# Order of the transposes and place of one division in a banded attention, on one Trainium2 core

## Chip, cores and metric

The kernel runs on one core of one Trainium2 chip. The metric is the device time of one execution in microseconds (us); for several runs their median is given. TensorE does the matrix products and the transposes, VectorE (DVE) and ScalarE (ACT) work on their results, GpSimd (POOL) does some of the splitting, and SyncE (SP) issues most of the loads.

## What is computed

A trunk of two layers over a prompt of 2048 positions and a sample of 512, with 1024 channels. The first layer is an attention in a window: every block of 128 queries sees its own block of keys and the two beside it, as far as they exist. The change lies in this layer:

```python
scores = einsum('bnqhgd,bnkhd->bnhgqk', qb, kw) * scale + bias      # three key blocks per query block
scores = where(mask, scores, -inf)
m = maximum(max(scores), sink)
p = exp(scores - m)
p = p / (sum(p) + exp(sink - m))
o = einsum('bnhgqk,bnkhd->bqnhgd', p, v)
x = x + (o * silu(gate)) @ w_out
```

The second layer mixes by a Fourier transform over positions and channels. It takes no part in the change.

## The kernel before

**Chunks.** The attention works in five chunks of 512 positions (`CHUNKS`, L35): chunk 0 is the whole sample, chunks 1 to 4 are the quarters of the prompt. Each chunk has four query blocks (0 to 3) and eight head pairs. A block has three key blocks (384 keys), except at an end of its sequence, where it has two (256 keys, `span`, L460). Block 0 is narrow in chunks 0 and 1, block 3 in chunks 0 and 4. For chunk 0 the weights are loaded in float32, split into a high and a low part (a cast on ScalarE, L121, and a subtraction on GpSimd, L126) and stored for the later chunks.

**Periods.** The loop of L851 runs n from 0 to 16; I call one pass a period. In period n one head pair and one pair of blocks is new (the lower pair, blocks 0 and 1, in even periods, the upper pair, blocks 2 and 3, in odd ones), and that of period n - 1 is old. The instructions of an engine follow a written order for those that go through `seq` and `pe` (L140 to L147); others, such as the weight casts, the squares for the next chunk's norm (L169) and the scaling of a projection (L299), have no written place, and a scheduler puts them between. In a period:

- TensorE makes the scores of one new block, `one`, into the banks `spt[0]` and `spt[1]` (L472), transposes the probabilities of an old block (`transp`, L517), makes the scores of the other new block, `two`, into `spt[2]` and `spt[3]`, and transposes the second old block. Then come projection matmuls for later head pairs (L95, as many as `quota`, L829, says) and the products of probabilities and values (`av`, L557).
- The transposes write two banks, one for each half of the queries. The block that is transposed second (an odd `b`) writes one half into `spt[0]` (L525), so it must wait until the new block's first scores have been read from there.
- VectorE adds bias to scores and takes the minimum on the way (`biased`, L491), makes the reciprocal of the sums (L507), divides three of the four heads (L511 in the prompt's chunks, L515 in chunk 0), makes the low part of the transposed probabilities (L540), and evicts projections and outputs (L410, L575).
- ScalarE makes the exponentials (`exps`, L499), divides the fourth head (L509), copies the transposed probabilities (`parts`, L539), and makes the first half of an eviction (L409 for queries, L566 for outputs).

**Order of the blocks.** `one` is the narrower block of the pair (L867 to L869), so the upper pair of chunks 0 and 4 is scored as 3, 2. The transposes and copies take the pair as 2, 3 all the same. ScalarE's division is that of the second head of the even block (L508): of the block scored first in most pairs, but of the one scored second in those upper pairs.

The queries of a head pair are evicted in odd periods, behind the divisions (L409 on ScalarE, then L410 on VectorE), and the next period's scores need them.

The functions that the change touches, with the profile's line numbers:

Of the kernel before, what the change touches and what calls it, by code (L numbers as in the profile page):

```python
# [42 lines left out]
def encoder(  # L43
# [33 lines left out]
    def bank(name):  # L77
        return banks[-1].tile([P, 512], F32, tag="bank", name=name)
# [61 lines left out]
    def seq(engine, ins):  # L140

        after(ins, chain.get(engine))
        chain[engine] = ins
        return ins

    def pe(ins):
        return seq(PE, ins) if PE in chain else ins  # L147

    def attention_phase():

        with ExitStack() as es:
# [88 lines left out]
            ps = bank("idle")  # L240
# [193 lines left out]
            def attention(c, p, res, uTs):  # L434
# [25 lines left out]
                def span(b):  # L460
                    gb = tok // P + b
                    k0 = 1 if tok + b * P == lo_t else 0
                    k1 = 2 if tok + (b + 1) * P == hi_t else 3
                    return gb, k0, k1
# [35 lines left out]
                        s[:, e0:e1], s[:, e0:e1], AF.Exp, bias=s[:, 386:387], scale=-1.0, accum_out=s[:, 387:388]  # L500
                    ))

                def divide(b, j):
                    gb, k0, k1 = span(b)
                    s = st[b, j]
                    ks, den = slice(1 + k0 * P, 1 + k1 * P), s[:, 387:388]
                    seq(DVE, DVE.reciprocal(den, den))  # L507
                    if j > b % 2:  # L508
                        seq(ACT, ACT.activation(s[:, ks], s[:, ks], AF.Copy, scale=den))  # L509
                    elif c:  # L510
                        seq(DVE, DVE.tensor_scalar(s[:, ks], s[:, ks], den, None, ALU.mult))  # L511
                    else:


                        seq(DVE, DVE.tensor_scalar(s[:, ks], s[:, ks], den, None, ALU.mult, ALU.add, accum_out=s[:, 386:387]))  # L515

                def transp(b):  # L517

                    gb, k0, k1 = span(b)
                    ss = [st.pop((b, j)) for j in range(2)]  # L520
                    if b % 2 == 0:
                        st["pts"] = ap.tile([P, 2, 2, 3, 2, P], F32R, align_bytes=LINE, tag="pt", bufs=1, name=f"pts{c}_{p}_{b}")
                    ps = [bank(f"pt{c}_{p}_{b}_{h}")[:, :384] for h in range(2 - b % 2)]
                    if b % 2:
                        ps.append(spt[0][:, 2:386])  # L525
                    ps = st["pt", b] = [t.rearrange("p (k j q) -> p k j q", k=3, j=2) for t in ps]
                    for j in range(2):
                        for kb in range(k0, k1):
                            for h in range(2):
                                rows = slice(64 * h, 64 * h + 64)  # L530
                                pe(PE.transpose(  # L531
                                    ps[h][:, kb, j, :], ss[j][rows, 1 + kb * P : 1 + (kb + 1) * P], ident[rows, rows]
                                ))
# [55 lines left out]
                def width(b):  # L589
                    gb, k0, k1 = span(b)  # L590
                    return k1 - k0

                return start, sinks, width, scores, biased, exps, divide, transp, parts, av, out_evac

            def out_proj(c, uTs):
# [198 lines left out]
            for c in range(len(CHUNKS)):  # L794
# [40 lines left out]
                def extra(i):  # L835
                    nonlocal norm_steps, invb, inv
                    if c + 1 < len(CHUNKS):
                        if i == 24:
                            norm_steps = stats(c + 1)
                        if i >= (38 if c else 24) and i % (2 if c else 4) == 0 and norm_steps:  # L840
                            inv = norm_steps.pop(0)()
                        elif i == 56:
                            invb = spread(c + 1, inv)
                    if c in EXTRA and i in EXTRA[c]:
                        EXTRA[c][i]()
                    if c == len(CHUNKS) - 1 and i in AHEAD:
                        AHEAD[i]()
                    if c == 0 and i % 8 == 3 and 1 <= i // 8 < 3:
                        load_w(0, LATE[i // 8 - 1], f"late{i // 8}", late=last_exp[0])

                for n in range(17):  # L851
                    new = (at[n // 2], 2 * (n % 2)) if n < 16 else None
                    old = (at[(n - 1) // 2], 2 * ((n - 1) % 2)) if n else None
                    behind = None
                    if c == 0 and n in (8, 10):

                        fetches[n // 2 + 2]()
                        behind = last_fetch[0]
                    if n % 2 == 0 and n < 14:
                        at[n // 2 + 1].start(behind)  # L860
                    if n % 2 and n // 2 + 2 < 8:
                        loads[n // 2 + 2]()
                    chain.setdefault(PE, None)

                    if new:

                        one, two = new[1], new[1] + 1  # L867
                        if new[0].width(two) < new[0].width(one):
                            one, two = two, one  # L869
                        new[0].scores(one, spt[:2])  # L870
                    if old:
                        old[0].transp(old[1])
                    if new:
                        for j in range(2):
                            new[0].biased(one, j)
                        new[0].scores(two, spt[2:])
                    if old:
                        old[0].transp(old[1] + 1)
                    if n == 15:

                        for j in range(2):
                            new[0].biased(two, j)
                    if old:
                        for b in range(2):
                            old[0].parts(old[1] + b)
                    if new:
                        for j in range(2):
                            new[0].exps(one, j)
                    if split and c:
                        split()  # L890
                        split = None
                    if new:
                        if n < 15:
                            for j in range(2):
                                new[0].biased(two, j)
                        while late:
                            late.pop()()
                        new[0].divide(one, 0)
                        for j in range(2):
                            new[0].exps(two, j)  # L900
                        new[0].divide(one, 1)
                        for j in range(2):
                            new[0].divide(two, j)
                    for i in range(quota[2 * n] if n < 15 else 18 - n):
                        (work or op).pop(0)()
                    if split:
                        split()
                        split = None
                    if old:
                        old[0].av(old[1])  # L910
                        split = old[0].out_evac(old[1])
                    if n % 2 and n < 15:
                        at[n // 2 + 1].sinks()
                    for i in range(4 * n, 4 * n + 4):
                        extra(i)
                    if n == 16:
                        split()
                    half = quota[2 * n + 1] if n < 14 else 4 if n == 14 else 2
                    for i in range(half):
                        (work or op).pop(0)()  # L920
# [770 lines left out]


    fourier_phase(attention_phase())


# [96 lines left out]
```

## Time and profile before

| | |
|---|---|
| median of three runs | 1588.2 us (1588.07 to 1588.9) |
| profiled execution | 1587.64 us |
| its span (first to last instruction) | 1585.9 us |
| granted TensorE clock, mean | 0.999 of full speed |
| instructions | 27430 |
| HBM read, written | 280.84 MB, 91.26 MB |

Times in the profile are microseconds from the start of the span unless marked ns. PE is TensorE's matrix products and PEld its weight loads, which overlap them. A row of the timeline gives start, duration, engine, line, operation, the tiles as out<-in, shape and count, and in brackets how long the engine had been idle and what ended that. A row of the waits gives who waited for whom, the sum in us, how often, and the longest wait. Matrix products are pipelined and their ends are modelled, so the shares of TensorE say little about short waits; the starts of instructions do.

### The profile page before, as it was taken

To read this page: it belongs to the slowest core of one execution; us is meant where nothing else is said; L and a number is where in the kernel's file an instruction comes from. 1 tells how busy PE (TensorE), PEld (TensorE's weight loads), DVE (VectorE), ACT (ScalarE), POOL (GpSimd) and SP (SyncE) were. 2 spreads that over 40 slices of the span, in tenths; PEclk is the share of its full clock that TensorE was granted. 3 is DMA by queue.
4 is the path that set the end of the run, shared out by engine and by line. 5 is a ranking of instruction groups with operands and counts; after the bars stand their busy time and mean duration, and the time that the engine had idled before them with its cause. 6 is when DMAs were issued, how large, how long until landed. Compare 5 with 4: busy or idle time off the path is not lost. (4 is left out here: it accounts for less than half of the span.)

```text
span 1585.9 us, 27430 instructions
## 1 busy us (share of the span) xinstructions
PE 1572.4 (99%) x9743; PEld 1320.2 (83%) x9743; DVE 1151.0 (73%) x2785; ACT 876.4 (55%) x2089; POOL 446.5 (28%) x613
## 2 busy tenths in 40 slices
PE   9999999999999999999999999999999999999998
PEld 7778888888898888988888888888888888888886
DVE  5788665887548786378764577669878878889796
ACT  6688634677237684257852476646655554343342
POOL 2566651421403414024222242223112111111110
PEclk9999999999999999999999999999999999999999
DMA  7587696665865567656649656675557469548752
GB/s 288 205 311 282 237 350 211 228 237 199 294 224 205 208 249 257 238 196 229 242 168 334 217 209 225 247 252 199 207 200 262 176 224 406 180 173 313 265 205 80
DMA packets 100579, 373.88 MB, mean 236 GB/s; under 512 B 12139, under 2 KB 22379, under 8 KB 83036
## 3 DMA queue, kind: packets, MB, share of 16 engines
q1 hardware_dynamic: 81708, 297.91, 52.8%
q0 software_dynamic: 16400, 70.04, 11.5%
q10 hardware_dynamic: 2336, 4.20, 0.7%
q8 instruction: 77, 1.26, 0.3%
q14 instruction: 58, 0.48, 0.1%
HBM read 280.84 MB, written 91.26 MB: 235 GB/s over the span
## 5 line engine op out<-in xcount | busy, mean ns | idle before, releaser
L95 PE MATMUL gp<-h,wg 128*128 128x512 f32 x960 | 237.7, 396 | 0.0
L95 PE MATMUL qp<-h,wq 128*128 128x512 f32 x960 | 237.2, 396 | 0.0
L491 DVE CUSTOM_DVE_ANT_0 S<-spt,b 128x385 f32<-128x385 f32 (+1 forms) x320 | 156.5, 528 | 103.7 <-PE spt L472 69.2
L95 PEld LDWEIGHTS gp<-h,wg 128*128 128x128 f32 x960 | 174.9, 188 | 37.3 <-issue 1.0
L95 PEld LDWEIGHTS qp<-h,wq 128*128 128x128 f32 x960 | 174.9, 188 | 36.7 <-issue 0.3
L499 ACT ACTIVATE S<-S 128x385 f32<-128x385 f32 (+1 forms) x320 | 188.8, 596 | 21.0 <-DVE S L491 20.6
L539 ACT CAST pts<-pt 128x384 fp32r<-128x384 f32 (+1 forms) x240 | 101.4, 461 | 166.2 <-PE pt L531 157.5
L540 DVE TENSOR_TENSOR pts<-pt,pts 128x384 fp32r<-128x384 f32 (+1 forms) x240 | 114.7, 524 | 20.5 <-ACT pts L539 19.5
L581 POOL TENSOR_TENSOR uT<-o,uT 128x256 fp32r<-128x256 f32 x75 | 55.6, 741 | 233.1 <-ACT uT L580 233.0
L95 PE MATMUL spt<-wo,uT 128*128 128x512 f32 x480 | 120.4, 391 | 0.0
L472 PE MATMUL spt<-kwin,qab 64*128 64x384 f32 (+1 forms) x960 | 119.1, 353 | 1.2 <-ACT qab L409 0.6
L95 PE MATMUL op<-wo,uT 128*128 128x512 f32 x480 | 118.9, 391 | 0.0
L557 PEld LDWEIGHTS av<-pts,v 128*128 128x128 f32 x576 | 101.3, 188 | 19.2 <-DVE pts L540 0.4
L557 PE MATMUL av<-pts,v 128*128 128x512 f32 (+1 forms) x576 | 116.0, 341 | 0.1
L95 PE MATMUL fo<-wo,tTu 128*128 128x512 f32 x480 | 115.2, 392 | 0.0
L95 PEld LDWEIGHTS op<-wo,uT 128*128 128x128 f32 x480 | 89.4, 188 | 18.5
L95 PEld LDWEIGHTS spt<-wo,uT 128*128 128x128 f32 x480 | 89.1, 188 | 18.4
L95 PEld LDWEIGHTS fo<-wo,tTu 128*128 128x128 f32 x480 | 88.3, 188 | 17.1
L511 DVE TENSOR_SCALAR S<-S 128x384 f32<-128x384 f32 (+1 forms) x192 | 96.0, 500 | 6.8
L472 PEld LDWEIGHTS spt<-kwin,qab 64*128 64x128 f32 x960 | 74.8, 186 | 30.0 <-issue 25.0
L577 POOL TENSOR_TENSOR o<-o,s 128x256 f32<-128x256 f32 x75 | 55.4, 738 | 137.4 <-DVE o L575 137.1
L531 PE MATMUL pt<-ident,S 64*128 64x64 f32 x1344 | 81.8, 222 | 0.0
(321 smaller groups left out, 3185.8 us busy)
## 6 DMA issues: line engine op xcount, KB each, us to landing
wo<-wsd SPq DMA_DIRECT2D x32, 1024.0 KB, 5.6
wq<-wsd SPq DMA_DIRECT2D x31, 1024.0 KB, 7.4
wg<-wsd SPq DMA_DIRECT2D x31, 1024.0 KB, 5.7
x<-x1d SPq DMA_DIRECT2D x40, 512.0 KB, 3.4
b<-b21d SPq DMA_DIRECT2D x40, 512.0 KB, 6.3
b<-rowd SPq DMA_DIRECT2D x40, 384.0 KB, 4.3
xs<-in_x_dram SPq DMA_DIRECT2D x23, 512.0 KB, 6.7
s2d<-gt POOLq DMA_DIRECT2D x40, 256.0 KB, 5.0
```

The source lines that it names most:

```text
L95: pe(PE.matmul(out, a[i], b[j], start=start and i + j == 0, stop=stop and i == 1, skip_group_check=more))
L472: pe(PE.matmul(banks[j][:, 2 + k0 * P : 2 + k1 * P], res["q"][rows, qp, b * P : (b + 1) * P], kwin[g][rows, kp, b * P + k0 * P : b * P + k ...
L491: seq(DVE, DVE.tensor_tensor_reduce(out=s[:, e0:e1], in0=ps[:, 1 + e0 : 1 + e1], in1=st["bias"][:, j, 386 - e1 : 386 - e0][:, ::-1], scale ...
L499: last_exp[0] = seq(ACT, ACT.activation(s[:, e0:e1], s[:, e0:e1], AF.Exp, bias=s[:, 386:387], scale=-1.0, accum_out=s[:, 387:388]))
L511: seq(DVE, DVE.tensor_scalar(s[:, ks], s[:, ks], den, None, ALU.mult))
L531: pe(PE.transpose(ps[h][:, kb, j, :], ss[j][rows, 1 + kb * P : 1 + (kb + 1) * P], ident[rows, rows]))
L539: seq(ACT, ACT.copy(hi, ps[:, k0:k1]))
L540: seq(DVE, DVE.tensor_tensor(lo, ps[:, k0:k1], f32(hi), ALU.subtract))
L557: pe(PE.matmul(to, v, pt, start=n == part == 0, stop=part == 1 and n in (1, len(todo) - 1), skip_group_check=n > 1,))
L577: eng.tensor_tensor(o, o, s, ALU.mult)
L581: low = eng.tensor_tensor(lo, o, f32(hi), ALU.subtract)
```

## The change

The order in which the blocks of a pair are scored is computed once for the new and for the old pair. Transposes and copies of the old pair follow it. Which block shares `spt[0]` no longer depends on its parity but on whether it is transposed second. ScalarE divides the second head of the block scored first, whatever its parity. Only pairs whose second block is the narrower one differ in what is done: the upper pairs of chunks 0 and 4, eight in each.

```diff
-                def divide(b, j):
+                def divide(b, j, act=False):
...
-                    if j > b % 2:
+                    if act:
                         seq(ACT, ACT.activation(s[:, ks], s[:, ks], AF.Copy, scale=den))
...
-                def transp(b):
+                def transp(b, second):
...
-                    if b % 2 == 0:
+                    if not second:
                         st["pts"] = ap.tile([P, 2, 2, 3, 2, P], F32R, align_bytes=LINE, tag="pt", bufs=1, name=f"pts{c}_{p}_{b}")
-                    ps = [bank(f"pt{c}_{p}_{b}_{h}")[:, :384] for h in range(2 - b % 2)]
-                    if b % 2:
+                    ps = [bank(f"pt{c}_{p}_{b}_{h}")[:, :384] for h in range(2 - second)]
+                    if second:
                         ps.append(spt[0][:, 2:386])
...
+                    order, older = [], []
+                    for at_b, pair in ((new, order), (old, older)):
+                        if at_b:
+                            pair += sorted((at_b[1], at_b[1] + 1), key=at_b[0].width)
...
                     if new:
-
-                        one, two = new[1], new[1] + 1
-                        if new[0].width(two) < new[0].width(one):
-                            one, two = two, one
+                        one, two = order
                         new[0].scores(one, spt[:2])
                     if old:
-                        old[0].transp(old[1])
+                        old[0].transp(older[0], 0)
...
-                        old[0].transp(old[1] + 1)
+                        old[0].transp(older[1], 1)
...
-                        for b in range(2):
-                            old[0].parts(old[1] + b)
+                        for b in older:
+                            old[0].parts(b)
...
-                        new[0].divide(one, 1)
+                        new[0].divide(one, 1, True)
```

## Prediction

> **What bounds the kernel now.** I read the page first, then busy time by stage, then the start of every period of the attention loop, then who waited for whom.
>
> ```profile
> PE 1572.4 (99%) x9743; PEld 1320.2 (83%) x9743; DVE 1151.0 (73%) x2785; ACT 876.4 (55%) x2089; POOL 446.5 (28%) x613
> ```
>
> TensorE is the bound, but "busy" hides waits: a matmul that is held counts as running. Only chunks 0 (512 sample positions, first) and 4 (last quarter of the prompt) have a narrower upper pair, so only there does the change do anything. Their busy times by stage:
>
> ```profile
> core 0: us, PE busy (x) PEld busy (x) DVE busy (x) ACT busy (x) POOL busy (x), PEclk, DMA share, GB/s
> 43.00:172.00 129.00, 127.04 (x891) 102.45 (x887) 107.28 (x385) 104.81 (x270) 75.80 (x110) 1.00 0.72 258
> 892.00:1016.00 124.00, 124.00 (x911) 102.56 (x910) 95.39 (x308) 87.89 (x241) 41.27 (x58) 1.00 0.59 212
> ```
>
> Chunk 4 (second row) has TensorE busy throughout. In chunk 0 it falls 1.96 us short, VectorE is 83% busy and ScalarE 81%. How much is really lost there comes from the starts of the score matmuls, one set per period (the loop index n of L851):
>
> ```profile
> 48.38 0.63 PE L472 MATMUL spt<-kwin,qab 64*128 64x256 f32 x6
> 56.96 0.62 PE L472 MATMUL spt<-kwin,qab 64*128 64x256 f32 x6
> 65.56 0.62 PE L472 MATMUL spt<-kwin,qab 64*128 64x256 f32 x6
> ...
> 168.87 0.71 PE L198 MATMUL spt<-ident,inv 128*128 128x128 f32 x5
> 172.29 0.62 PE L472 MATMUL spt<-kwin,qab 64*128 64x256 f32 x6
> ...
> 1564.83 2.72 PE Wo L95 x12
> ```
>
> Periods 1 and 2 take 8.58 and 8.60 us; I take 8.59 as a period without waits. By the quota of L829 eleven of periods 1 to 14 hold 24 projection matmuls and three hold 21; at 2.72/12 = 0.227 us each the short ones need 7.91. Period 14 holds five small transposes more (at most 0.71). So 11 x 8.59 + 3 x 7.91 + 0.71 = 118.9 us are needed and 172.29 - 48.38 = 123.9 are taken: **5.0 us are lost in chunk 0's loop**. The waits of this stretch name the place:
>
> ```profile
> DVE qab L410 <- ACT qab L409: 8.4, 7, 1.4
> ACT S L509 <- DVE S L507: 7.6, 11, 1.6
> PEld spt L531 <- DVE S L491: 1.9, 7, 0.3
> PEld spt L472 <- ACT qab L409: 1.6, 2, 1.0
> ```
>
> Seven times VectorE waits for ScalarE's half of the query eviction, which is queued behind ScalarE's division (L509), which waits for VectorE's reciprocal (L507). TensorE then waits in two places: scores for qab, and transposes for the biased add that must first read the bank they share.
>
> **The change part by part.** In odd periods block 3 (256 keys) is scored before block 2 (384 keys). Before, ScalarE divides block 2's second head, the last thing ready; after, block 3's, and VectorE takes the wide one. Rows at the seam of periods 3 and 4, all engines:
>
> ```profile
> 71.36 0.19 ACT L499 ACTIVATION_READ_ACCUMULATOR S<-S 128x1 f32 x1
> 71.55 0.16 DVE L507 RECIPROCAL S<-S 128x1 f32<-128x1 f32 x1
> 71.74 0.62 DVE L515 TENSOR_SCALAR_CACHE_REDUCE S<-S 128x384 f32<-128x384 f32 x1
> ...
> 72.47 0.62 ACT L509 ACTIVATE S<-S 128x384 f32<-128x384 f32 x1 [0.93 <-DVE S L507]
> 73.00 0.58 ACT L409 ACTIVATE qab<-qp 128x512 fp32r<-128x512 f32 x1
> 73.61 0.69 DVE L410 SCALAR_TENSOR_TENSOR qab<-qp,qab 128x512 fp32r<-128x512 f32 x1 [1.17 <-ACT qab L409]
> 73.89 0.58 ACT L566 COPY t<-av 64x512 f32<-64x512 f32 x1
> 74.35 0.39 PE L472 MATMUL spt<-kwin,qab 64*128 64x256 f32 x2 [0.22 <-DVE qab L410]
> 74.57 0.85 DVE L575 TENSOR_TENSOR o<-av,t 64x256 f32<-64x256 f32 x2 [0.28 <-ACT b L454]
> ...
> 75.45 0.43 DVE L491 CUSTOM_DVE_ANT_0 S<-spt,b 128x257 f32<-128x257 f32 x1
> 75.94 0.27 PE L531 MATMUL spt<-ident,S 64*128 64x64 f32 x1
> ```
>
> And the narrow forms, from the groups by form:
>
> ```profile
> L515 DVE TENSOR_SCALAR_CACHE_REDUCE S<-S 128x256 f32<-128x256 f32 x24 | 11.4, 476 | 0.4
> L509 ACT ACTIVATE S<-S 128x256 f32<-128x256 f32 x8 | 4.0, 504 | 1.0 <-DVE S L507 1.0
> ```
>
> *ScalarE.* After the last exponential (71.36 + 0.19 = 71.55) it now has block 3's division at once, since that reciprocal no longer stands behind block 2's: 71.55 to 72.05. The query eviction L409 moves from 73.00 to about 72.0, L566 from 73.89 to 72.9: 0.9 to 1.0 us earlier (the 0.93 of idle time and 0.11 of width).
>
> *VectorE.* Block 3's second division goes (0.476) and block 2's comes (0.62 by the 71.74 row): +0.14 us in each of eight periods, 1.1 us in all. It fills part of the 1.17 us that VectorE sat before L410, so it is hidden; without that cover it costs its 1.1 us. By my walk VectorE now divides until 72.7, L410 runs to 73.35, L575 from 73.6 to 74.45, L491 from 74.45 instead of 75.45.
>
> *TensorE.* The third score pair (held until 74.35, 0.5 us after its turn) finds qab ready. The second set of transposes stood still until the add of 75.45 had read the bank (75.94); now that add ends near 74.9 and the transposes reach it near 74.8, so about 0.1 us remains of 0.35. Counts and shapes on TensorE stay: 8 + 12 transposes become 12 after 8. The block transposed first no longer hangs on ScalarE's last division; the second set now needs VectorE's wide one (ended 72.7 by the walk), two microseconds before its turn, and behind it stand only projection matmuls. The order of the copies (L539, L540) follows; same counts. Period 4 so falls by about 0.9 us. The same holds at the seams before periods 8 and 12; in periods 6, 10 and 14 only the bank wait is there to lose, in 7 and 11 what ScalarE brings late.
>
> *What the scheduler moves along.* The built program's instruction order shows that ScalarE's free-standing work changes place in chunk 0: the squares of the next chunk's norm (L169) leave the place ahead of the division; the ones met in periods 7, 8 and 10 now stand ahead of the next period's copies (L539), and that of period 11 stands between the division and L409. Two weight casts (L121) come between the two pairs of exponentials in periods 8 and 10, one waits ahead of the copies of period 12, one in period 13 goes from ahead of the division to behind it, and the gate-weight cast of period 7 goes behind the copies, which frees the matmuls with the values there. What such a place costs:
>
> ```profile
> 118.69 1.04 ACT L121 CAST wg<-w32g 128x1024 fp32r<-128x1024 f32 x1
> 120.14 0.65 ACT L539 CAST pts<-pt 128x256 fp32r<-128x256 f32 x2 [0.40 <-PE pt L531]
> ...
> L169 ACT ACTIVATE xs<-xs x5: 1042/1044/1046, 106.9 to 141.5; 128x1024 f32<-128x1024 f32 x5
> L169 ACT ACTIVATION_READ_ACCUMULATOR xs<-xs x5: 183/186/188, 107.8 to 142.5; 128x1 f32 x5
> ```
>
> A square takes 1.04 + 0.19 us. After period 8 it takes the place of a cast of 1.04 that today leaves 0.40 spare; but the periods get shorter and the cast comes earlier in the same period. Walking periods 8 to 11 by these durations, ScalarE ends its value copy (L566) 0.2 to 0.5 us too late in periods 9 and 11. Bounds: nothing, and 3 x 1.23 + 3 x 1.04 = 6.8 us if each moved piece held TensorE for its length. I take 0.8, near the low end, because the total of ScalarE's work does not grow. With 0.1 at the other seams, 1.1 us of the 5.0 stay. GpSimd's weight splits follow the casts; SP's loads in chunk 0 keep their order. In chunk 4 three weight loads on SP's queue go ahead of loads that only the next phase uses; TensorE's work in the loop covers that, and I cost it at nothing.
>
> *Chunk 4.* Its periods hold no wait to remove. Against it stands a thin margin; here chunk 1's mirrored pair and chunk 4's:
>
> ```profile
> 279.62 0.78 PE L472 MATMUL spt<-kwin,qab 64*128 64x384 f32 x6
> 288.43 0.62 PE L472 MATMUL spt<-kwin,qab 64*128 64x256 f32 x6
> ...
> 901.27 0.78 PE L472 MATMUL spt<-kwin,qab 64*128 64x384 f32 x6
> 902.20 0.56 DVE L491 CUSTOM_DVE_ANT_0 S<-spt,b 128x385 f32<-128x385 f32 x1 [1.28 <-PE spt L472]
> 902.84 0.26 PE L531 MATMUL spt<-ident,S 64*128 64x64 f32 x1
> 910.04 0.62 PE L472 MATMUL spt<-kwin,qab 64*128 64x256 f32 x6
> ```
>
> The add ends at 902.76, the transposes that need its bank begin at 902.84. With 8 instead of 12 ahead of them they arrive about 0.1 us sooner and wait. Chunk 1 already runs that order (narrow first): its period is 8.81 against 8.77, so +0.04 x 8 = 0.3 us.
>
> *Sum:* -5.0 + 1.1 + 0.3 = -3.6 us. The profiled execution took 1587.64 us (span 1585.9), so 1584.0; the median, 0.56 above it, becomes **1584.6**. A measurement here tells a change from none at about 0.2%, 3.2 us, so the forecast lies just beyond it.
>
> **Weighed against the Trainium skill.** "Perfetto Trace Analysis", section "Optimizing Scalar/DVE Operations", says that a saturated DVE is a reason to hand work to Scalar; this change does the reverse. The 83% of chunk 0 agrees that VectorE is near full, and by that rule the 1.1 us above would be added: -2.5 us. It is rival B below, whose working needs no page.
>
> **The rivals.**
> A. *The gain is swallowed between chunks 0 and 1.* There the transfers set the pace:
>
> ```profile
> 213.55 0.35 SPq L117 DMA_DIRECT2D wk<-wsd  x1
> ...
> wk<-wsd SPq DMA_DIRECT2D x2, 1024.0 KB, 8.3
> ...
> 218.32 11.04 PE L95 MATMUL spt<-h,wk 128*128 128x512 f32 x48
> ```
>
> The second key weight lands near 213.55 + 8.3 = 221.9; TensorE wants it after 24 of the 48 matmuls, 218.32 + 24 x 0.227 = 223.8. If the transfers kept their clock, 3.6 us earlier would meet a wall after 1.9: -1.9, **1586.3**. Against: their issues hang on buffers that TensorE frees, so they move along.
> B. *VectorE becomes the bound of chunk 0*: its 1.1 us is not covered, **1585.7**. For: 83% busy. Against: its 1.17 us waits sit exactly there.
> C. *Only one half works.* The bank waits (1.9 us by the waits' row) stay, since L575 and L491 may stay late behind ScalarE: -3.6 + 1.9 = -1.7, **1586.5**.
> D. *Slower.* The moved squares and casts hold TensorE whole: -5.0 + 6.8 + 0.3 + 1.1 = +3.2, **1591.4**. It decides once ScalarE is some 1.2 us behind in periods 8 to 11; the trace shows it 81% busy and 0.40 us in hand. If only two thirds are exposed it is level with before.
>
> **How the numbers follow.** Forecast, 1583.2 to 1585.4 (waits left between 0.3 and 2): 0.60. A 0.10, B 0.10, C 0.12, D 0.08. Range 1582.9 (all 5.0 gone, nothing for chunk 4) to 1586.8 (beyond C): only D lies outside, with the tails of the others. Faster by over 0.2% means below 1585.0: most of the forecast's band and a little of B, 0.57; slower by over 0.2% (above 1591.4): 0.04; the rest 0.39.
>
> **What would show it.** Right: periods 4, 8 and 12 of chunk 0 near 8.6 to 8.8 us; L409 directly behind a 256-wide L509; VectorE's wait before L410 under half of 8.4; the wait of L531 for L491 near 0.5 in chunk 0; chunk 1's first scores some 3 to 4 us earlier and the phases after it as long as today; chunk 4's periods 8.77 to 8.81. Wrong: new waits of TensorE in periods 8 to 12 behind L169 or L121 (D), an unchanged start of chunk 1 (A), VectorE without idle time before L410 (B).

## The result, and the profile after

The changed kernel takes **1585.98 us** (median of 22 runs, 1584.36 to 1589.24) against 1588.18 us before (median of 22 runs, 1586.33 to 1591.17): ratio 0.9987, 95% interval 0.9981 to 0.9993. It is faster, by 2.2 us or 0.13%, which lies within the 0.2% that the prediction counted as the same. The forecast of 1584.6 was 1.4 us too low. The time lies above the band of 1583.2 to 1585.4 to which the prediction gave 0.60, and inside its range of 1582.9 to 1586.8. By the number alone rival B (1585.7) would have been nearer than the forecast; what decides between them are the starts of the periods and the experiments.

The profiled execution took 1585.16 us with a span of 1583.4 us, so the spans differ by 2.5 us. The page's row of busy times hardly shows it; the two stages in which the change acts show more. The page of the changed kernel (busy us, share of the span, instructions):

```profile
PE 1570.8 (99%) x9743; PEld 1321.0 (83%) x9743; DVE 1153.8 (73%) x2785; ACT 872.8 (55%) x2089; POOL 446.6 (28%) x613
```

Its busy times by stage (window, its length, then PE, PEld, DVE, ACT and POOL with their instructions):

```profile
43.00:172.00 129.00, 128.61 (x931) 105.23 (x928) 110.78 (x395) 105.07 (x276) 78.17 (x113) 1.00 0.72 261
892.00:1016.00 124.00, 124.00 (x908) 101.91 (x907) 96.77 (x307) 85.35 (x240) 39.07 (x54) 1.00 0.56 206
```

In chunk 0 (first row) TensorE now falls 0.39 us short of the window instead of 1.96. VectorE is 86% busy. In chunk 4 TensorE reads as full as before, 124.00 of 124.00 us, although, as the starts will show, the loop has become 0.85 us longer. A matmul that is held counts as running in this view, so a wait in the middle of a row of transposes leaves no trace in it.

The starts of the periods in the changed kernel (score matmuls of `one`, timeline of TensorE):

```profile
48.48 0.63 PE L472 MATMUL spt<-kwin,qab 64*128 64x256 f32 x6
...
73.61 0.62 PE L472 MATMUL spt<-kwin,qab 64*128 64x256 f32 x6
82.68 0.62 PE L472 MATMUL spt<-kwin,qab 64*128 64x256 f32 x6
...
107.81 0.62 PE L472 MATMUL spt<-kwin,qab 64*128 64x256 f32 x6
116.94 0.62 PE L472 MATMUL spt<-kwin,qab 64*128 64x256 f32 x6
...
133.43 0.63 PE L472 MATMUL spt<-kwin,qab 64*128 64x256 f32 x6
142.52 0.62 PE L472 MATMUL spt<-kwin,qab 64*128 64x256 f32 x6
...
168.90 0.62 PE L472 MATMUL spt<-kwin,qab 64*128 64x256 f32 x6
...
251.73 1.15 PE L472 MATMUL spt<-kwin,qab 64*128 64x256 f32 x12
...
882.09 1.33 PE L472 MATMUL spt<-kwin,qab 64*128 64x384 f32 x12
...
1013.99 0.62 PE L472 MATMUL spt<-kwin,qab 64*128 64x256 f32 x6
```

The last three of these starts in the kernel before:

```profile
255.12 1.15 PE L472 MATMUL spt<-kwin,qab 64*128 64x256 f32 x12
...
885.39 1.33 PE L472 MATMUL spt<-kwin,qab 64*128 64x384 f32 x12
...
1016.44 0.62 PE L472 MATMUL spt<-kwin,qab 64*128 64x256 f32 x6
```

Chunk 0's loop (periods 1 to 14) takes 168.90 - 48.48 = 120.42 us, before 123.91: 3.49 us are won. The loop starts 0.10 us later than before and so ends 3.39 us earlier. Chunk 1's first scores start at 251.73 instead of 255.12, so all of these 3.39 us pass the boundary between the chunks; 0.09 of them are lost on the way to chunk 4. Chunk 4's loop (periods 0 to 14) runs from 882.09 to 1013.99, 131.90 us; before it ran from 885.39 to 1016.44, 131.05 us: 0.85 us are given back. 3.30 - 0.85 = 2.45 us is what the spans show.

Three periods of chunk 0 are still long: period 4 (73.61 to 82.68) 9.07, period 8 9.13 and period 11 9.09 us, against 8.59 without waits. That is 0.5 us in each, 1.5 us in all. The waits of the stretch, changed kernel:

```profile
ACT S L509 <- DVE S L507: 1.3, 5, 0.3
PEld spt L531 <- DVE S L491: 0.8, 3, 0.3
DVE qab L410 <- ACT qab L409: 0.7, 3, 0.3
```

VectorE's wait for the query eviction fell from 8.4 to 0.7 us, ScalarE's wait for the reciprocal from 7.6 to 1.3, and TensorE's waits for the query eviction are gone. What is left in these rows is the bank wait, three times instead of seven; its 0.8 us are about half of the 1.5, since a matmul that is held counts as running. The seam of periods 3 and 4, to be laid beside that of before:

```profile
66.60 0.37 ACT L539 CAST pts<-pt 128x256 fp32r<-128x256 f32 x1 [1.17 <-PE pt L531]
66.87 1.05 ACT L121 CAST wq<-w32q 128x1024 fp32r<-128x1024 f32 x1
...
68.82 1.08 ACT L121 CAST wg<-w32g 128x1024 fp32r<-128x1024 f32 x1
...
71.97 0.51 ACT L509 ACTIVATE S<-S 128x256 f32<-128x256 f32 x1
72.36 0.60 ACT L409 ACTIVATE qab<-qp 128x512 fp32r<-128x512 f32 x1
73.08 0.69 DVE L410 SCALAR_TENSOR_TENSOR qab<-qp,qab 128x512 fp32r<-128x512 f32 x1
...
73.97 0.85 DVE L575 TENSOR_TENSOR o<-av,t 64x256 f32<-64x256 f32 x2 [0.20 <-ACT b L454]
74.84 0.43 DVE L491 CUSTOM_DVE_ANT_0 S<-spt,b 128x257 f32<-128x257 f32 x1
75.33 0.27 PE L531 MATMUL spt<-ident,S 64*128 64x64 f32 x1
```

L409 stands directly behind the narrow division, as the change intends. But the first add (L491) starts 74.84 - 73.61 = 1.23 us behind the scores, and the transposes that need its bank wait for its end at 75.27. And ScalarE sat idle for 1.17 us before its first copy and only then made the query-weight cast. The same cast in the timeline of before:

```profile
65.09 1.04 ACT L121 CAST wq<-w32q 128x1024 fp32r<-128x1024 f32 x1
```

There it lay in ScalarE's idle time, ahead of the copies. The gate-weight cast (68.82) stands ahead of the exponentials in both kernels.

### The profile page after: what moved, and what is told of

The parts are those of the page before. It is cut to its first block, busy times and chain, and to the rows that moved or that the text cites. A ratio compares the mean times of both kernels' runs of the same rounds, so it can differ in the third digit from the quotient of the medians.

```text
span 1583.4 us, 27413 instructions
## 1 busy us (share of the span) xinstructions
PE 1570.8 (99%) x9743; PEld 1321.0 (83%) x9743; DVE 1153.8 (73%) x2785; ACT 872.8 (55%) x2089; POOL 446.6 (28%) x613
## 5 line engine op out<-in xcount | busy, mean ns | idle before, releaser
L491 DVE CUSTOM_DVE_ANT_0 S<-spt,b 128x385 f32<-128x385 f32 (+1 forms) x320 | 156.6, 529 | 110.7 <-PE spt L472 65.8
L95 PE MATMUL op<-wo,uT 128*128 128x512 f32 x480 | 118.9, 392 | 0.0
L531 PEld LDWEIGHTS pt<-ident,S 64*128 64x128 f32 x1312 | 78.4, 138 | 4.4 <-issue 2.0
```

The source lines that it names most:

```text
L95: pe(PE.matmul(out, a[i], b[j], start=start and i + j == 0, stop=stop and i == 1, skip_group_check=more))
L491: seq(DVE, DVE.tensor_tensor_reduce(out=s[:, e0:e1], in0=ps[:, 1 + e0 : 1 + e1], in1=st["bias"][:, j, 386 - e1 : 386 - e0][:, ::-1], scale ...
L531: pe(PE.transpose(ps[h][:, kb, j, :], ss[j][rows, 1 + kb * P : 1 + (kb + 1) * P], ident[rows, rows]))
```

## The experiments

Chunk 0's loop and chunk 4's loop are read from the starts of the score matmuls, as above; "without waits" is the 118.9 us of the prediction.

| kernel | chunk 0's loop | chunk 4's loop | time: ratio to before, or us beside before in the same series |
|---|---|---|---|
| before | 123.91 | 131.05 | |
| changed | 120.42 | 131.90 | 0.9987 (0.9981 to 0.9993) |
| 1 chunk 0 only | 120.55 | 130.86 | 0.9975 (0.9966 to 0.9985) |
| 2 division only | 120.34 | 131.06 | 0.9979 (0.9969 to 0.9989) |
| 3 transposes only | 124.94 | 131.81 | 1590.61 (one run), before 1588.82 |
| 4 less VectorE | 119.96 | 131.82 | 1584.82 (one run), before 1588.82 |
| 5 sinks on VectorE | 121.57 | 131.13 | 1584.67 (one run), before 1587.56 |
| 6 casts pinned | 121.42 | 131.84 | 1586.95 (one run), before 1587.56 |
| 7 division, casts pinned | 120.48 | 131.00 | 0.9988 (0.9979 to 0.9997) |
| 8 as 7, sink copy later | 118.99 | 131.05 | 0.9969 (0.9958 to 0.9981) |
| 9 changed, all pinned | 119.07 | 131.85 | 0.9977 (0.9968 to 0.9986) |

The loops tell more than the times. In chunk 4 the five kernels with the old order of the transposes (before, 1, 2, 7, 8) take 130.86 to 131.06 us, and five with the new order (changed, 3, 4, 6, 9) 131.81 to 131.90. The times of experiments 1, 2, 3 and 9 lie 0.1 to 0.7 us outside the bands that were named for them; where there is an interval (1, 2 and 9), it covers the band.

Three theories were set against each other. **M**: the gain is the division's alone, and the order of the transposes costs chunk 4 its margin. **V**: what chunk 0 still loses comes from VectorE's longer chain. **S**: it comes from casts that ScalarE makes at the wrong place.

### 1. The change in chunk 0 only

```diff
+                    if old and c:
+                        older.sort()
                     if old:
                         old[0].transp(older[0], 0)
...
-                        new[0].divide(one, 1, True)
+                        act = min(order) if c else one
+                        new[0].divide(one, 1, act == one)
                         for j in range(2):
-                            new[0].divide(two, j)
+                            new[0].divide(two, j, j == 1 and act == two)
```

> The change in chunk 0 alone; chunk 4 keeps the old order of transposes and copies and the old place of the division. Theory M (chunk 4 pays because only 8 instead of 12 transposes stand ahead of the shared bank's need): chunk 0's loop stays at 120.4 us as in the changed kernel, chunk 4's loop falls from 131.9 back to 131.05, even periods from 8.9 to 8.77, and the time is 3.3 to 3.5 us under before, near 1584.8. Rival (chunk 4 is longer for another reason, such as the loads moved ahead on SyncE's queue or its shifted start): chunk 4 stays at 131.9 and the time at 2.5 us under before.

Measured: 1584.64 us against 1588.82 (medians of 10 and 19 runs), 4.2 us less where 3.3 to 3.5 were expected; chunk 0's loop 120.55, chunk 4's 130.86. The timeline of its first even period, in this kernel:

```profile
897.96 0.79 PE L472 MATMUL spt<-kwin,qab 64*128 64x384 f32 x6
898.58 0.53 PE L531 MATMUL pt<-ident,S 64*128 64x64 f32 x12
898.89 0.56 DVE L491 CUSTOM_DVE_ANT_0 S<-spt,b 128x385 f32<-128x385 f32 x1 [1.27 <-PE spt L472]
899.54 0.25 PE L531 MATMUL spt<-ident,S 64*128 64x64 f32 x1
906.73 0.62 PE L472 MATMUL spt<-kwin,qab 64*128 64x256 f32 x6
```

And in the changed kernel, whose scores start at 897.96 as well:

```profile
898.58 0.41 PE L531 MATMUL pt<-ident,S 64*128 64x64 f32 x8
898.88 0.56 DVE L491 CUSTOM_DVE_ANT_0 S<-spt,b 128x385 f32<-128x385 f32 x1 [2.10 <-PE pt L531]
899.51 0.28 PE L531 MATMUL spt<-ident,S 64*128 64x64 f32 x1
906.86 0.62 PE L472 MATMUL spt<-kwin,qab 64*128 64x256 f32 x6
```

The add runs at the same moment in both, and so do the transposes that need its bank. But from there 11 transposes are still to be made in the changed kernel and 8 in this one, and the period takes 8.90 instead of 8.77 us. This is M. The shifted start drops out as a cause, since chunk 4 starts at 882.09 in both kernels. The loads on SyncE's queue do not drop out by this run alone, for their order went back with the rest: here a load of `w32B` (967.05) is issued ahead of one of `wg` (973.79), in the changed kernel behind it (974.90 and 974.53). They drop out by experiment 5, which keeps the changed kernel's order (974.03, then 974.41) and loses the stall all the same.

### 2. The division only

```diff
+                    if old:
+                        older.sort()
                     if old:
                         old[0].transp(older[0], 0)
```

> ScalarE divides the second head of the block scored first, but transposes and copies keep the order 2, 3. Theory M: the gain belongs to the division alone. The waits for the query eviction are gone, and 12 transposes ahead of the shared bank hide some 0.3 us more at the seams of periods 4 and 8: chunk 0's loop 119.8 to 120.4 us (before 123.9, changed 120.4), chunk 4's loop 131.05, the time 3.4 to 4.0 us under before. Rival H (both halves are needed, since block 2, ready last, is now transposed first): TensorE waits in front of the first transposes for the wide division, and chunk 0's loop stays above 121.5.

Measured: 1585.57 us against 1588.82 (10 and 19 runs), 3.25 us less where 3.4 to 4.0 were expected; chunk 0's loop 120.34, chunk 4's 131.06. The whole gain is there without the order of the transposes, and chunk 4 pays nothing: M. H falls. In detail the loop is not the changed kernel's: period 4 takes 8.61 and period 11 8.83 us, but periods 7 and 8 take 8.98 and 9.48. Rows of ScalarE in this kernel, at periods 3 and 7:

```profile
64.94 1.05 ACT L121 CAST wq<-w32q 128x1024 fp32r<-128x1024 f32 x1
66.36 0.65 ACT L539 CAST pts<-pt 128x256 fp32r<-128x256 f32 x2 [0.37 <-PE pt L531]
...
105.29 1.05 ACT L169 ACTIVATE xs<-xs 128x1024 f32<-128x1024 f32 x1
106.33 0.50 ACT L509 ACTIVATE S<-S 128x256 f32<-128x256 f32 x1
```

Here the query-weight cast of period 3 comes ahead of the copies and period 4 is on time, while a square (L169) got ahead of the division of period 7 and period 8 is late. The two kernels differ only in the order of the transposes and copies; the rest is where free-standing work fell. That led to experiments 6 to 9.

### 3. The transposes only

```diff
-                        new[0].divide(one, 1, True)
+                        act = min(order) if True else one
+                        new[0].divide(one, 1, act == one)
                         for j in range(2):
-                            new[0].divide(two, j)
+                            new[0].divide(two, j, j == 1 and act == two)
```

> Transposes and copies follow the order of the scores, but the division stays with block 2's second head, the last one ready. Theory M: nothing is won. VectorE's 8 us of waiting for the query eviction stay, chunk 0's loop is 123.9 to 124.8 us (before 123.9), chunk 4's loop 131.9, and the time is 0.9 to 1.7 us above before. Rival H (both halves carry a share): chunk 0's loop 122.5 or less.

Measured: 1590.61 us against 1588.82 (one run of this kernel), chunk 0's loop 124.94, chunk 4's 131.81. The wait for the query eviction in this kernel is that of before:

```profile
DVE qab L410 <- ACT qab L409: 8.4, 7, 1.4
```

Alone, the order of the transposes makes both chunks longer, by 1.03 and 0.76 us; chunk 0 came out 0.14 above the band named. M, by the loops of one execution.

### 4. Less work for VectorE

```diff
                         for j in range(2):
-                            new[0].divide(two, j)
+                            if j == 0 or c or n % 2 == 0:
+                                new[0].divide(two, j)
```

> In chunk 0's upper pairs the second head of the block scored second is not divided at all (left out: a reciprocal of 0.16 and a division of 0.62 us on VectorE in each of eight periods), all else as in the changed kernel. It asks what holds the 0.5 us that periods 4 and 8 still lose. Theory V (VectorE's longer chain of divisions): periods 4 and 8 fall from 9.07 and 9.13 to 8.6, chunk 0's loop to 119.4 us. Theory S (ScalarE, with two weight casts ahead of the exponentials, ends the query eviction and the value copy late, and VectorE can only follow): both stay at 8.95 to 9.1, the loop at 120.1 to 120.4.

This kernel leaves out a division that the result needs; only its times are of use. Measured: period 4 9.09 us, period 8 8.66, chunk 0's loop 119.96. V fits the second, S the first, so the rows have to speak. The bounds of period 4 in this kernel:

```profile
73.42 0.62 PE L472 MATMUL spt<-kwin,qab 64*128 64x256 f32 x6
82.51 0.62 PE L472 MATMUL spt<-kwin,qab 64*128 64x256 f32 x6
```

ScalarE's gate-weight cast of period 7, in this kernel:

```profile
102.41 1.05 ACT L121 CAST wg<-w32g 128x1024 fp32r<-128x1024 f32 x1
```

The same cast in the changed kernel:

```profile
103.10 1.05 ACT L121 CAST wg<-w32g 128x1024 fp32r<-128x1024 f32 x1 [0.66 <-DMA w32g<-in_w_in_dram]
```

Period 4 did not gain anything from 0.78 us less on VectorE: V falls there. In period 7 the cast waited 0.66 us for its load in the changed kernel and came 0.7 us sooner in this execution, and with it the exponentials and all that stands behind them on ScalarE. VectorE was not what held period 8: its output eviction (L575), behind which the first add stands, waits for ScalarE's sink copy (L454) in both kernels, 0.27 us in the changed one and 0.28 here, and starts 0.69 us behind the start of ScalarE's value copy (L566) in both. What differs is the load: SyncE issued it at 90.66 in the changed kernel and at 89.76 here. Why it was issued sooner, and whether the lighter VectorE had a part in that, stays open; experiments 6 and 9 show that less work on VectorE isn't needed.

### 5. The sink copy on VectorE

```diff
-                    ends = ACT.copy(
+                    ends = (DVE.tensor_copy if c else ACT.copy)(
...
-                        seq(ACT, ends)
+                        seq(DVE if c else ACT, ends)
```

> The changed kernel, with the copy of the sink values into the bias tile made by VectorE instead of ScalarE in chunks 1 to 4, so that the first biased add of a head pair waits for one engine (TensorE) and no longer for ScalarE's copy as well. Theory T (in chunk 4's even periods that add starts 0.1 us later than in chunk 1's narrow pair, 0.92 against 0.82 us behind the start of the scores, only because it waits on two engines, and this is what 8 transposes don't cover): the add starts 0.82 behind, even periods of chunk 4 fall from 8.88-8.93 to 8.77-8.81, its loop from 131.9 to 131.0 us. Rival (the wait itself, not the number of waits, is what costs): even periods stay at 8.9, the loop at 131.9.

Measured: chunk 4's loop 131.13, its even periods 8.78 to 8.81. The add of period 2 in this kernel, its scores at 898.05:

```profile
898.87 0.56 DVE L491 CUSTOM_DVE_ANT_0 S<-spt,b 128x385 f32<-128x385 f32 x1 [1.51 <-PE spt L472]
```

It starts 0.82 us behind the scores, not 0.92, and the stall is gone with 8 transposes ahead. So T's times came, and with ScalarE's copy out of the add's way the missing tenth is gone. T's reason, the number of waits, is not shown: an instruction of VectorE's queue that only waits stands ahead of the add in this kernel too (at 897.40, 1.45 us before the add; in the changed kernel it ends 0.09 us before it). Not expected: chunk 0's loop grew to 121.57, because the copy for chunk 1's first head pair now stood in VectorE's queue in period 14 and waited there for that pair's bias load (period 14 took 10.18 us):

```profile
DVE b L454 <- DMA b<-rowd: 1.5, 1, 1.5
```

### 6. Gate-weight casts and squares at fixed places

```diff
                     if n % 2 and n // 2 + 2 < 8:
-                        loads[n // 2 + 2]()
+                        loads[n // 2 + 2](*(() if c else ("q", chain[ACT])))
...
                         at[n // 2 + 1].sinks()
+                    if c == 0 and n % 2 and n // 2 + 2 < 8:
+                        loads[n // 2 + 2]("g", chain[ACT])
...
-                            after(sq, last_exp[0])
+                            after(sq, chain[ACT] if c else last_exp[0])
```

`load` takes one of the two weights here, and its cast (L121) is made to follow the instruction given. 

> The changed kernel, with ScalarE's free-standing work given a place in chunk 0: the query-weight cast of an odd period behind the value copy of the period before, the gate-weight cast behind the value copy and the sink copy at the odd period's end, and the squares behind the value copy, so that the gate-weight cast no longer stands ahead of the exponentials. Theory S (periods 4, 8 and 11 lose 0.5 us each because two casts stand ahead of the exponentials of the period before, one of them waiting for its load): periods 4, 8 and 11 fall from 9.07, 9.13 and 9.09 to 8.6-8.7, chunk 0's loop from 120.4 to 118.9-119.4 us. Theory V (VectorE's longer chain): they stay near 9.1, the loop at 120.4. Not known: period 12, which takes three pieces of 1.05 to 1.23 us ahead of its copies; if they hold it, its successor grows by up to 0.5.

Measured: periods 8 and 11 fell from 9.13 and 9.09 to 8.59 and 8.61, period 4 only to 8.86. Period 13, the successor of period 12, grew from 8.57 to 8.79. The loop as a whole grew to 121.42, for period 14 took 11.23 us instead of 9.18. S is right for two of the three seams; the third had still the query-weight cast behind the first copy, as in the changed kernel.

### 7. Division alone, casts and squares at fixed places

This is experiment 2 with the edit of experiment 6.

> The version that the runs point to: only ScalarE's division moves, transposes and copies keep the order 2, 3, and the casts and squares of chunk 0 have their places as in the run before. By theories M and S: chunk 0's loop 118.9 to 119.3 us, chunk 4's 131.05, the time 4.6 to 5.0 us under before, about 1583.4. Rival (the casts only move the lateness to the copies of the even periods): chunk 0's loop 120 or more and the time 3.5 us under before.

Measured: 1585.52 us against 1587.56 (11 and 15 runs), 2.0 us less where 4.6 to 5.0 were expected. Periods 1 to 12 are all 8.56 to 8.59 or, the short ones, 7.90 to 7.92 us, but period 13 is 8.78 and period 14 10.76: the loop 120.48. So most of the further gain was there and was lost again in one period. Its cause, ScalarE in this kernel:

```profile
162.11 0.20 ACT L455 COPY b<-sk 128x4 f32<-128x4 f32 x1 [4.34 <-DMA b<-rowd]
162.33 1.14 ACT L540 CAST pts<-pt 128x384 fp32r<-128x384 f32 x3
```

ScalarE reached the sink copy for chunk 1's first head pair early and waited 4.34 us for its bias load, with the copies of the transposed probabilities behind it.

### 8. The same with the sink copy behind the last value copy

```diff
                     if p:
                         seq(ACT, ends)
+                    else:
+                        after(ends, last_evac[0])
```

> As the run before (division alone, casts and squares of chunk 0 in fixed places), and the copy of the sink values for the next chunk's first head pair goes behind the last value copy of the chunk, so that ScalarE no longer waits 4.3 us in period 14 for that pair's bias load with the copies of the transposed probabilities queued behind it. If that wait is what made period 14 10.76 us: period 14 is 9.1 to 9.2, chunk 0's loop 118.8 to 119.1 us, the gain carries on to chunk 1's first scores, and the time is 4.6 to 5.2 us under before. Rival (the period is long because the work that was moved earlier has nowhere to go): period 14 stays above 10 us and the time at 3 us under before.

Measured: **1582.64 us** against 1587.82 (7 and 11 runs), 5.2 us less: faster than before, and by its ratio (0.9969 beside 0.9987) than the changed kernel too. Starts in this kernel:

```profile
48.21 0.63 PE L475 MATMUL spt<-kwin,qab 64*128 64x256 f32 x6
...
158.00 0.62 PE L475 MATMUL spt<-kwin,qab 64*128 64x256 f32 x6
167.20 0.62 PE L475 MATMUL spt<-kwin,qab 64*128 64x256 f32 x6
```

Period 14 is 9.20 us, chunk 0's loop 118.99: the wait of the sink copy was the cause.

### 9. The changed kernel with the query and gate casts in ScalarE's written order

```diff
-        ACT.copy(w[:, 0], w32)
+        up = ACT.copy(w[:, 0], w32)
+        if behind:
+            seq(ACT, up)
```

and the edits of experiments 6 and 8 on the changed kernel.

> The changed kernel whole (transposes follow the scores), with chunk 0's casts in the written order of ScalarE, so that the query-weight cast of an odd period comes ahead of the copies and not behind the first of them, the gate-weight cast and the squares as in the pinned runs, and the sink copy behind the chunk's last value copy. Theory S (the lateness of periods 4, 8 and 11 is the place of casts alone, and 8 transposes ahead of the shared bank are enough in chunk 0): periods 4, 8 and 11 are 8.6 us, chunk 0's loop 118.9 to 119.2, chunk 4's loop stays 131.9, and the time is 4.0 to 4.4 us under before. Rival (8 transposes instead of 12 leave period 4 late whatever ScalarE does): period 4 stays at 8.85 as in the run with only the gate-weight casts moved, the loop at 119.2 to 119.6.

Measured: 1583.94 us against 1587.45 (11 and 15 runs), 3.5 us less where 4.0 to 4.4 were expected. ScalarE at periods 2 and 3 in this kernel:

```profile
65.09 1.04 ACT L121 CAST wq<-w32q 128x1024 fp32r<-128x1024 f32 x1
66.37 0.65 ACT L544 CAST pts<-pt 128x256 fp32r<-128x256 f32 x2 [0.23 <-PE pt L536]
```

The bounds of period 4 in this kernel:

```profile
73.36 0.62 PE L477 MATMUL spt<-kwin,qab 64*128 64x256 f32 x6
81.94 0.62 PE L477 MATMUL spt<-kwin,qab 64*128 64x256 f32 x6
```

Period 4 is 8.58 us, 8 and 11 are 8.59 and 8.60, the loop 119.07. The order of the transposes and VectorE's divisions are the changed kernel's, and none of the three seams is late: S is right, its rival and V fall. Period 13 stays 0.2 us longer than in the changed kernel (8.78), as in every kernel with the casts moved. For period 4 two casts were moved, the gate-weight cast (experiment 6, 9.07 to 8.86) and then the query-weight cast too (8.58 here); the second alone was not tried. Between experiments 8 and 9 chunk 0 differs by 0.08 us and chunk 4 by 0.80: that is what the order of the transposes and copies costs.

## Why the prediction was right, and what it mis-sized

- **5.0 us are lost in chunk 0's loop: right.** Experiment 8 runs the same matmuls in 118.99 us; 118.9 were reckoned.
- **The division frees the query eviction: right, and it is the whole gain.** These markers came: L409 directly behind a 256-wide L509, VectorE's wait before L410 0.7 of 8.4 us, TensorE no longer held for queries. Of the other markers, period 12 came (8.63), periods 4 and 8 did not (9.07 and 9.13), the wait for L491 fell to 0.8 and not to 0.5, and chunk 4's even periods are 8.88 to 8.93 and not 8.77 to 8.81. Experiments 2 and 3 divide the credit: division alone -3.57 us in chunk 0, transposes alone +1.03. The prediction had priced the two halves as one.
- **Waits that stay in chunk 0, 1.1 us: mis-sized and at the wrong place.** It was 1.5 us, in periods 4, 8 and 11, where the walk had 9 and 11. Periods 4, 8 and 12 were to fall by about 0.9 us each and fell by 0.48, 0.41 and 0.59; period 7 gave the most, 1.06, and period 11 became 0.24 longer. The step that failed is the list of what the scheduler moves along, and what its pieces cost. It had the casts and squares of periods 7 to 13, but not the query-weight cast of period 3, which went behind the first copy: ScalarE's division, by the walk at 71.55, came at 71.97, and period 4 at 9.07 and not at 8.6 to 8.8. It had the gate-weight cast of period 7, but as a help; in the trace it stands ahead of the exponentials, waits 0.66 us for its load, and period 8 behind it is 0.54 us too long. With the casts and squares moved (experiment 9) periods 4, 8 and 11 lose nothing.
- **Chunk 4, 0.3 us: mis-sized, 0.85.** The mechanism was right (8 transposes in place of 12 reach the bank too soon). The price was read from chunk 1's mirrored pair, where the add starts 0.82 us behind the scores; in chunk 4's even periods it is the first add of a head pair, has ScalarE's sink copy to wait for as well and starts 0.91 to 0.93 us behind them (experiment 5). The seven even periods of the loop with an old pair grew by 0.08 to 0.15 us each, where 0.04 was reckoned.
- **The sum:** -3.49 + 0.85, with the 0.10 us of the later start and the 0.09 lost before chunk 4, is -2.45 instead of -3.6. Both terms that were too small err to the same side, so nothing cancelled; that the time lies in the range owes much to its width.
- **A fell:** all of the 3.39 us by which chunk 0's loop ends earlier pass into chunk 1.
- **B was half right in its sign and wrong in its cause.** At the seam before period 4 VectorE has no idle time before L410, as B's marker has it (73.08 stands directly behind the division). But VectorE was not the bound: with 0.78 us less of work period 4 stayed long, and with casts at other places its loss vanished with the same work. The Trainium skill's rule ("Perfetto Trace Analysis", section "Optimizing Scalar/DVE Operations": a saturated DVE is a reason to hand work to Scalar), as the prediction applied it, would have charged this change 1.1 us. VectorE is 86% busy in chunk 0, and experiment 9 leaves no room for that charge: its loop takes 119.07 us with all of VectorE's divisions, beside 118.9 reckoned without any wait.
- **C fell in its reason:** by the waits' rows 0.8 of 1.9 us of bank waits stayed, through ScalarE as C says, but through the place of casts and not through the halves of the change. Its heading, that only one half works, holds in another sense than it was priced: the division does all of the work, and the order of the transposes costs. That was no rival of mine.
- **D fell:** no piece held TensorE for its length; the largest loss of the changed kernel was 0.54 us in a period.

## What to carry to other kernels

When a change has two halves, ask of each alone what it gains: here one half held all of the gain and the other was a cost, and they were priced as one. A margin of a tenth of a microsecond between two engines must be read at the very instruction concerned and not at a mirrored one, since one more wait of 0.1 us was enough to use it up. And look through all of the instructions that a scheduler places freely, in all periods: giving the casts of 1.05 us and one sink copy their place won a further 1.35 us in chunk 0's loop (120.42 to 119.07 in experiment 9), beside 3.49 for the change.

## What the runs showed of the hardware

In chunk 4 of the changed kernel the first biased add of a head pair starts 0.91 to 0.93 us behind the start of its scores in the even periods 2 to 14, and 0.82 in period 0. In the even periods 2 to 14 an instruction of VectorE's queue that only waits ends 0.08 to 0.09 us before the add; in period 0 it ends 2.77 us before it. The row of period 2:

```profile
L491 DVEq EVENT_SEMAPHORE  x1: 21/21/21, 898.8 to 898.8; - x1
```

In experiment 5 such an instruction stands there in the same seven periods, but it ends 0.95 to 1.67 us before the add, and the add starts 0.82 us behind the scores in each of them. So the tenth goes with a waiting instruction that ends just ahead of the add, and not with the presence of one; what each of them waits for the trace does not say.

The gate-weight cast of period 7 waited for its load in three executions with the same work in chunk 0 up to there (0.66, 0.80 and 0.76 us in the changed kernel and in experiments 1 and 5), and period 8 took 9.13, 9.29 and 9.23 us. In experiment 4 it did not wait, and period 8 took 8.66. Where a seam hangs on a load's landing, one execution does not give its price to better than the 0.16 us between these three.
